# Probabilities turned in float32r after a copy by DMA, and weight sums formed on loading, in a two-layer encoder on one Trainium2 core

## The chip, the cores and the metric

The kernel runs on one NeuronCore of one Trainium2 chip. The metric is the device time of one execution in microseconds (us), median over runs. TensorE (PE) multiplies and transposes and its weight loads are shown as PEld; VectorE (DVE), ScalarE (ACT) and GpSimd (POOL) work on elements; SyncE (SP) issues most transfers, POOL the others, and 16 DMA engines carry them out. SP's transfers run on the queue that the profile calls hardware_dynamic (q1), POOL's on software_dynamic (q0).

## The reference, cut to what matters

Two layers, sequence 1024, width 1024, all in float32.

```python
def block_attention(q, k, v, scale):          # in 128-query blocks
    s = jnp.einsum('bqhgd,bkhd->bhgqk', qi, k) * scale
    p = jax.nn.softmax(s, axis=-1)
    return jnp.einsum('bhgqk,bkhe->bqhge', p, v)

def conv_gated_ffn(h, w_up, conv_w, conv_b, w_down):
    a = h @ w_up                              # 1024 x 1024 by 1024 x 5632
    a = ap[:, :-2] * conv_w[0] + ap[:, 1:-1] * conv_w[1] + ap[:, 2:] * conv_w[2] + conv_b
    gate, val = a[..., :D_FF], a[..., D_FF:]
    return (jax.nn.silu(gate) * val) @ w_down # 1024 x 2816 by 2816 x 1024

for l in range(DEPTH):
    x = x + hybrid_mixer(rms_norm(x), ...)    # 6 heads GQA, 6 heads MLA, gMLP, then w_out
    x = x + memory_cross_attention(rms_norm(x), mem, ...)
    x = x + conv_gated_ffn(rms_norm(x), ...)
return rms_norm(x)
```

## The kernel before, in words

All large products are made in float32r, which TensorE multiplies faster than float32 but with fewer bits. Each operand is therefore split into a rounded part (`hi`) and the rest (`lo`), and a product is the sum of three matmuls (hi hi, hi lo, lo hi). Work tiles are 46 slots of 128 x 1024 elements in the on-chip memory; `Slots` hands them out from a list, first in, first out, at the time the program is written, so the code's order decides which tile takes which slot. A tile that gets a slot waits until the last readers and writers of that slot's former tile are done. Each engine runs its instructions in the order of the code.

**Attention** (about 172 to 500 us in the first layer and 1550 to 1860 us in the second). There are 24 items in a layer, numbered 0 to 23: 12 heads by two halves of 512 queries. An item has four tiles of 128 queries by 1024 keys. The function `attention` runs one step for each tile. In step s of item i it issues: the scores of tile s (TensorE, L318 and L319, or L744 and L745) and their maximum (VectorE, L295); the scaling of the tile before by the reciprocal of its sum (POOL, L305); two `turn` calls for the item before; then the exponential of tile s (ScalarE, L299). `turn(k)` transposes the k-th 128 keys of all four tiles into one bank of the accumulator memory (TensorE, L140, four transposes by a float32 identity `ident`) and splits that bank (ScalarE hi, L123, VectorE lo, L124); `value(k)` multiplies the two parts with the values. With `LAG = 1` the first `turn` of an item comes one step after the step in which the scaling of its fourth tile is issued. Side work (`fill`) and transfers (`extra`, by item number) are placed between these.

**Weight sums.** The up and down products of the feed-forward are made by a scheme of seven products of half size in place of eight (Strassen's kind), numbered m = 1 to 7. The weight is stored as four blocks w0 to w3; products 1, 2 and 4 take a block as it is, and 5, 7, 6 and 3 take the sums w2+w3, w0+w2, w0+w2+w3 and w0+w1+w2+w3. In the kernel before, all four sums are formed in DRAM while attention runs: a copy on SP's queue (`copy`, L796) and an adding transfer on POOL's queue (`add`, L801), piece by piece, and the last additions for the down weights during the up projection (`add_later`).

**Up projection** (about 746 to 1165 us in the first layer). `order` lists (j, m): column block j of 22 and product m. For each the loop calls `fetch` (a 256 KB block into half a slot, SP, L1089), `make_w` (hi by ScalarE, L1096, lo by VectorE, L1097), `product` (12 matmuls, L1143 to L1145) and `post`. Fetching runs nine products ahead (`FETCH`) and splitting four (`AHEAD`). The convolution and gate follow in small steps (`todo`); `keep(j)` stores the result in DRAM (`gq`, SP, L1213) and forms the sums of row blocks by adding transfers on POOL's queue (L1216).

**Down projection.** `fetch_d` loads the block of kept rows and that of the weight, `make_d` splits both, `d_mm` multiplies (L1256).

Other lines named below: L110 is the rounding in `load` (POOL), L132 the power in `rstd` (POOL), L688 a sum over partitions with one moving column, L116 to L118 are the three matmuls of `mm3`.

Of the kernel before, what the change touches and what calls it, by code (L numbers as in the profile page):

```python
# [35 lines left out]
LAG = 1  # L36
WARM = 16
# [32 lines left out]
def trunk(ctx: ExitStack, tc: tile.TileContext, a: dict, out: bass.AP):  # L70
# [3 lines left out]
    stats = ctx.enter_context(tc.tile_pool(name="stats", bufs=24))  # L74
# [8 lines left out]

    def ins_of(i):
        return getattr(i, 'ins', i)
# [13 lines left out]
    ident = cpool.tile([P, P], F32, name="ident")  # L99
    ones = cpool.tile([P, 1], F32, name="ones")  # L100
# [34 lines left out]
    def transpose4(srcs):  # L135

        b = bank()
        for j, s in enumerate(srcs):
            m = s.shape[-1]
            nc.tensor.transpose(b[:m, j * P : (j + 1) * P], s, ident)  # L140
        return b
# [139 lines left out]
    class Item:  # L281
# [20 lines left out]
        def scale(self, t):  # L302
            p, r = self.ps[t], stat()
            nc.vector.reciprocal(r[:, 0:1], self.den[:, t : t + 1])  # L304
            Item.last = nc.gpsimd.tensor_scalar(p, p, r[:, 0:1], 0.0, ALU.mult, ALU.add)  # L305
# [78 lines left out]
    def layer(l, nt, w_m, last):  # L384
# [396 lines left out]
        class Blocks:  # L781

            def __init__(self, w, parts, name):
                self.w, self.parts, self.at = w, parts, [sum(parts[:i]) for i in range(len(parts))]
                self.sum = {
                    (m, i): dpool.tile([P, n * CH + 16], F32, tag=f"{name}{l}_{m}_{i}", name=f"{name}{l}_{m}_{i}")[:, : n * CH]
                    for m in (5, 6, 7, 3) for i, n in enumerate(parts)
                }  # L790
# [4 lines left out]
            def copy(self, m, i):  # L795
                c = nc.sync.dma_start(self.sum[m, i], self.piece({5: 2, 6: 0, 7: 0, 3: 1}[m], i))  # L796
                tc.add_manual_dep(ins_of(c), ins_of(Item.last).name, mybir.DependencyInfo(mybir.DependencyClass.Sync, mybir.DependencyReason.DATA), reason="not sooner")

            def add(self, m, i):
                src = self.sum[{6: 5, 3: 6}[m], i] if m in (6, 3) else self.piece({5: 3, 7: 2}[m], i)  # L800
                tc.keep_in_program_order(nc.gpsimd.dma_start(self.sum[m, i], src, accum_op=ALU.add))  # L801

            def block(self, m, j):
                if m in (1, 2, 4):
                    return self.w[{1: 0, 2: 1, 4: 3}[m]][:, j * CH : (j + 1) * CH]
                i = max(i for i in range(len(self.parts)) if self.at[i] <= j)
                return self.sum[m, i][:, (j - self.at[i]) * CH : (j - self.at[i] + 1) * CH]

            def steps(self):
                n = len(self.parts)  # L810
                return [(self, m, i + o) for i in range(0, n, 2) for m, o in ((5, 0), (5, 1), (7, 0), (6, 0), (6, 1), (7, 1), (3, 0), (3, 1)) if i + o < n]
# [5 lines left out]
        items += [mla(h, c) for h in range(MLA_H) for c in range(NC)]  # L817
        fill[0] += [lambda k=k: turn_cq(0, k) for k in range(2)] + [lambda: norm_low(1, ssq)]
# [51 lines left out]
        extra, steps = {}, w_u.steps()  # L870
        for n, (w, m, i) in enumerate(steps):
            g = n * 18 // len(steps)
            extra.setdefault(g, []).append(lambda w=w, m=m, i=i: w.copy(m, i))
            extra.setdefault(g + 3, []).append(lambda w=w, m=m, i=i: w.add(m, i))
        later = deque(sorted(w_d.steps(), key=lambda s: (5, 7, 6, 3).index(s[1])))
        for n, (w, m, i) in enumerate(later):
            extra.setdefault(n * 20 // len(later), []).append(lambda w=w, m=m, i=i: w.copy(m, i))

        def add_later():
            if later:  # L880
                w, m, i = later.popleft()
                w.add(m, i)
# [218 lines left out]
        for _ in range(FETCH - AHEAD):  # L1101
            fetch()
# [107 lines left out]
        def keep(j):  # L1210
# [4 lines left out]
            for q, p in ((("u3", "22"), ("u2", "u1"), ("u4", "u2")) if j % 2 else (("u1", "11"),)):  # L1215
                nc.gpsimd.dma_start(gq[q, i], gq[p, i], accum_op=ALU.add)  # L1216
# [6 lines left out]
        def fetch_d():  # L1223
            if (mi := next(d_fetch, None)) is not None:
# [3 lines left out]
                nc.sync.dma_start(quarter(z, 1), w_d.block(m, i))  # L1228
# [35 lines left out]
        def down(after0, after1, tail):  # L1264

            for m, i in d_order:
# [20 lines left out]
                for _ in range(2):  # L1287
                    if todo:
                        todo.popleft()()
                if i == NP - 1:  # L1290
# [8 lines left out]
        for i, (j, m) in enumerate(order):  # L1299
            for _ in range(1 + (i < AHEAD)):  # L1300
                fetch()
            for _ in range(1 + (i < AHEAD)):
                make_w()
# [6 lines left out]
            if m == 5 and j > 1:  # L1310
# [93 lines left out]
    nc.sync.dma_start(ident, a["ident"])  # L1404
    nc.sync.dma_start(colts[0], a["cols"][0])
# [96 lines left out]
```

## Time and profile before

| | |
|---|---|
| median of 3 runs | 2774.91 us (2772.91 to 2776.51) |
| the profiled execution | 2770.64 us, its span 2768.8 us |
| granted TensorE clock | 0.998 of full speed |
| busy share PE, PEld, DVE, ACT, POOL | 98%, 83%, 70%, 53%, 26% |
| DMA queues q1 (SP) and q0 (POOL) | 323.84 MB and 92.28 MB |
| transposes of `transpose4` (L140) | 2320, 324.0 us busy |

The span is the profiled execution from its first to its last instruction; all sums of durations are held against it. A row of groups reads: line, engine, operation, out<-in with buffer numbers left out, count, then busy us and mean ns of one. Matmul durations overlap, so the time from one start to the next is what a matmul costs in a row of them. The chain of waits is the path of work that ended last, followed back from the end. In the windows, each engine's busy us stand in a stretch of 50 us, then the granted clock, the DMA engines' mean busy share and GB/s. A slot is `s` in all rows; `u` and `d` are the weight sums in DRAM, `g` (also `g_u`) the kept rows, `stat` small columns, `bank` and `pair` accumulators.

### The profile page before, as it was taken

The numbers are of one execution on the slowest core, as the hardware profiler recorded it, in microseconds if no ns is written. First come the engines' busy times: TensorE is split into PE (matmuls) and PEld (weight loads), VectorE is DVE, ScalarE is ACT, GpSimd is POOL, SyncE is SP. The second block draws the span as 40 slices with busy tenths as digits, with TensorE's granted clock in tenths as the row PEclk, the third lists the DMA queues.
The fourth block names the chain that finished last, engine by engine and source line by source line (L and its number), as shares of the span: only waits on it lengthen the run. The fifth ranks groups of instructions, "written<-read, shape, count | busy, mean of one in ns | idle before, by whom it ended". The sixth has DMA issues, their size and how long they took to land.

```text
span 2768.8 us, 37951 instructions
## 1 busy us (share of the span) xinstructions
PE 2724.2 (98%) x13648; PEld 2284.4 (83%) x13648; DVE 1941.6 (70%) x2905; ACT 1470.8 (53%) x2838; POOL 706.3 (26%) x744
## 2 busy tenths in 40 slices
PE   9999999999999999999999999999999999999998
PEld 7997888888878888888889877888888888888887
DVE  5489879556697777774445888894666877778754
ACT  4378978224554444553333888881345544446432
POOL 3245676320001110000123456662200011100000
PEclk9999999999999999999999999999999999999999
DMA  4027994221159875785210289831221698767752
GB/s 147 27 80 199 263 233 97 73 69 62 46 150 237 223 213 166 225 272 183 88 59 19 83 232 265 220 83 61 70 68 46 173 239 225 204 169 244 247 187 102
DMA packets 160748, 418.80 MB, mean 151 GB/s; under 512 B 17840, under 2 KB 18480, under 8 KB 146224
## 3 DMA queue, kind: packets, MB, share of 16 engines
q1 hardware_dynamic: 137376, 323.84, 34.6%
q0 software_dynamic: 23040, 92.28, 18.2%
q8 instruction: 107, 1.75, 0.2%
q14 instruction: 81, 0.66, 0.1%
q10 hardware_dynamic: 144, 0.26, 0.0%
HBM read 371.75 MB, written 206.05 MB: 209 GB/s over the span
## 4 chain that ended last, share of the span: by engine, by line
PE 85%; DVE 5%; ACT 3%; DMA 3%; POOL 2%; issue 1%; SPq 0%; POOLq 0%; DVEq 0%; ACTq 0%
PE bank L1256 8%; PE bank L116 7%; PE bank L118 7%; PE bank L117 7%; PE bank L140 7%; PE pair L1256 6%; PE bank L1144 5%; PE bank L1145 5%; PE bank L1143 5%; PE pair L1143 4%; PE pair L1144 4%; PE pair L1145 4%; PE bank L318 3%; PE bank L319 3%; PE pair L116 2%; PE pair L118 2%
## 5 line engine op out<-in xcount | busy, mean ns | idle before, releaser
L124 DVE TENSOR_TENSOR s<-bank,s 128x512 fp32r<-128x512 f32 (+3 forms) x552 | 331.5, 630 | 116.4 <-ACT s L123 112.7
L116 PE MATMUL bank<-s,s 128*128 128x512 f32 (+4 forms) x1124 | 404.2, 360 | 4.6 <-DVE s L124 3.4
L118 PE MATMUL bank<-s,s 128*128 128x512 f32 (+4 forms) x1124 | 399.5, 356 | 1.1 <-DVE s L111 0.9
L117 PE MATMUL bank<-s,s 128*128 128x512 f32 (+4 forms) x1124 | 398.4, 355 | 0.3 <-DVE s L111 0.3
L123 ACT ACTIVATE s<-bank 128x512 fp32r<-128x512 f32 (+3 forms) x552 | 286.0, 556 | 205.7 <-PE bank L140 142.5
L140 PE MATMUL bank<-ident,s 128*128 128x128 f32 (+1 forms) x2320 | 324.0, 274 | 17.5 <-POOL s L305 6.3
L140 PEld LDWEIGHTS bank<-ident,s 128*128 128x128 f32 (+1 forms) x2320 | 270.1, 140 | 77.7 <-DVE s L124 9.6
L1096 ACT ACTIVATE s<-s 128x512 fp32r<-128x512 f32 x308 | 187.5, 627 | 181.5 <-PE bank L1145 46.1
L1144 PE MATMUL bank<-s,s 128*128 128x512 f32 x704 | 274.5, 390 | 0.9 <-DVE s L209 0.9
L1145 PE MATMUL bank<-s,s 128*128 128x512 f32 x704 | 273.9, 389 | 0.0
L1143 PE MATMUL bank<-s,s 128*128 128x512 f32 x704 | 273.7, 389 | 0.0
L305 POOL TENSOR_SCALAR s<-s,stat 128x1024 f32<-128x1024 f32 x192 | 222.8, 1160 | 184.4 <-DVE stat L304 136.5
L295 DVE TENSOR_REDUCE stat<-pair 128x1 f32<-128x1024 f32 x192 | 233.5, 1216 | 39.6 <-PE pair L118 19.0
L132 POOL TENSOR_TENSOR stat<-stat,mhalf 128x1 f32<-128x1 f32 (+3 forms) x94 | 84.3, 897 | 634.3 <-DVE stat L131 634.1
L1256 PE MATMUL bank<-s,s 128*128 128x512 f32 (+1 forms) x1068 | 242.7, 387 | 1.6 <-DVE stat L131 1.6
L116 PEld LDWEIGHTS bank<-s,s 128*128 128x128 f32 x1124 | 211.7, 189 | 33.6 <-DVE s L124 3.7
L1241 DVE TENSOR_TENSOR s<-s,s 128x512 fp32r<-128x512 f32 x264 | 170.6, 685 | 93.1 <-ACT s L1240 93.1
L1256 PEld LDWEIGHTS bank<-s,s 128*128 128x128 f32 x1068 | 198.7, 188 | 42.3 <-DVE x L1347 1.8
L118 PEld LDWEIGHTS bank<-s,s 128*128 128x128 f32 x1124 | 211.7, 188 | 26.3 <-DVE s L111 1.3
L117 PEld LDWEIGHTS bank<-s,s 128*128 128x128 f32 x1124 | 212.1, 189 | 24.1 <-DVE s L111 0.6
L1240 ACT ACTIVATE s<-s 128x512 fp32r<-128x512 f32 x264 | 153.9, 623 | 140.9 <-DMA s<-g_u 47.3
L1097 DVE TENSOR_TENSOR s<-s,s 128x512 fp32r<-128x512 f32 x308 | 201.7, 686 | 36.2 <-ACT s L1096 33.9
(182 smaller groups left out, 5521.0 us busy)
## 6 DMA issues: line engine op xcount, KB each, us to landing
s<-u SPq DMA_DIRECT2D x176, 256.0 KB, 4.3
u<-in_w_up SPq DMA_DIRECT2D x40, 1024.0 KB, 13.3
s<-in_w_up SPq DMA_DIRECT2D x132, 256.0 KB, 4.4
g_u<-s SPq DMA_DIRECT2D x88, 256.0 KB, 3.0
s<-g_u SPq DMA_DIRECT2D x88, 256.0 KB, 3.3
s<-d SPq DMA_DIRECT2D x88, 256.0 KB, 3.6
u<-in_w_up POOLq DMA_DIRECT2D x20, 1024.0 KB, 18.4
u<-u POOLq DMA_DIRECT2D x20, 1024.0 KB, 13.3
```

Of the source, the lines that this page charges most:

```text
L116: nc.tensor.matmul(o, l[0], r[0], start=first, stop=False)
L117: nc.tensor.matmul(o, l[0], r[1], start=False, stop=False)
L118: nc.tensor.matmul(o, l[1], r[0], start=False, stop=last)
L123: nc.scalar.activation(hi, src, AF.Copy)
L124: nc.vector.tensor_tensor(lo, src, f(hi), ALU.subtract)
L140: nc.tensor.transpose(b[:m, j * P : (j + 1) * P], s, ident)
L295: nc.vector.reduce_max(self.nm[:, 0:1], s, axis=AX.X, negate=True)
L305: Item.last = nc.gpsimd.tensor_scalar(p, p, r[:, 0:1], 0.0, ALU.mult, ALU.add)
L1143: nc.tensor.matmul(o, lh, rh, start=k == 0 and m in (1, 5, 6), stop=False, skip_group_check=True)
L1144: nc.tensor.matmul(o, lh, rl, start=False, stop=False, skip_group_check=True)
L1145: nc.tensor.matmul(o, ll, rh, start=False, stop=k == 3, skip_group_check=True)
L1256: nc.tensor.matmul(o, lh[p], rh[q], start=m in (1, 5, 2) and i == 0 and k == 0, stop=i == NP - 1 and k == 2, skip_group_check=True)
```

## The change

- In 18 of 24 items (`BY_DMA`: 0 to 10 and 17 to 23) the tiles t = 0, 1, 2 are copied, after scaling, by a transfer on SP's queue into a fresh slot of type float32r (512 KB, 54 in each layer). The old slot goes back to the list at once. Transposes of these tiles use the float32r identity `identr` and write float32r; the fourth tile of each item, and all tiles of items 11 to 16, stay float32.
- Of the weight sums only w0+w2+w3 (m = 6) is formed in DRAM, by a copy that is now on POOL's queue and two additions. Sums for m = 5, 7 and 3 are formed on loading: SP loads the first block (256 KB) and POOL issues an adding transfer of the second into the same half slot, 66 times in each up projection and 33 times in each down projection.
- Before the up projection `AHEAD` = 4 blocks are fetched in place of `FETCH - AHEAD` = 5. The adding transfers of `keep` are put off by 3, 6 and 9 products (`due`). `add_later` is called for even j only and has six additions in place of its earlier ones. The pool of small columns has 23 buffers in place of 24.

```diff
+BY_DMA = (*range(0, 11), *range(17, 24))
...
-    stats = ctx.enter_context(tc.tile_pool(name="stats", bufs=24))
+    stats = ctx.enter_context(tc.tile_pool(name="stats", bufs=23))
...
+    identr = cpool.tile([P, P], F32R, name="identr")
...
-            nc.tensor.transpose(b[:m, j * P : (j + 1) * P], s, ident)
+            o = b[:m, j * P : (j + 1) * P]
+            if s.dtype == F32R:
+                nc.tensor.transpose(o.bitcast(F32R), s, identr)
+            else:
+                nc.tensor.transpose(o, s, ident)
...
-            Item.last = nc.gpsimd.tensor_scalar(p, p, r[:, 0:1], 0.0, ALU.mult, ALU.add)
+            nc.gpsimd.tensor_scalar(p, p, r[:, 0:1], 0.0, ALU.mult, ALU.add)
+            if self.by_dma and t < TPC - 1:
+                w = self.ps[t] = sl.get()
+                nc.sync.dma_start(f(w), p)
+                sl.put(p)
...
-            def copy(self, m, i):
-                c = nc.sync.dma_start(self.sum[m, i], self.piece({5: 2, 6: 0, 7: 0, 3: 1}[m], i))
...
+            def copy(self, i):
+                tc.keep_in_program_order(nc.gpsimd.dma_start(self.sum[i], self.piece(0, i)))
+            def add(self, i, b):
+                tc.keep_in_program_order(nc.gpsimd.dma_start(self.sum[i], self.piece(b, i), accum_op=ALU.add))
...
+            def load(self, z, m, j):
+                first, *second = {1: (0,), 2: (1,), 4: (3,), 6: (4,), 5: (2, 3), 7: (0, 2), 3: (4, 1)}[m]
+                nc.sync.dma_start(z, self.col(first, j))
+                if second:
+                    nc.gpsimd.dma_start(z, self.col(second[0], j), accum_op=ALU.add)
...
+        for i in range(len(UP_PARTS)):
+            extra.setdefault(2 * i, []).append(lambda i=i: w_u.copy(i))
+            for n in range(2):
+                extra.setdefault(2 * i + 4 + 3 * n, []).append(lambda i=i, n=n: w_u.add(i, 2 + n))
+        for i in range(len(DOWN_PARTS)):
+            extra.setdefault(13 + 2 * i, []).append(lambda i=i: w_d.copy(i))
...
-                nc.sync.dma_start(raws[jm][0], w_u.block(jm[1], jm[0]))
+                w_u.load(raws[jm][0], jm[1], jm[0])
...
-        for _ in range(FETCH - AHEAD):
+        for _ in range(AHEAD):
             fetch()
...
-                nc.gpsimd.dma_start(gq[q, i], gq[p, i], accum_op=ALU.add)
+                due.append((step[0] + 3 + 3 * n, lambda q=q, p=p, i=i: nc.gpsimd.dma_start(gq[q, i], gq[p, i], accum_op=ALU.add)))
...
-                nc.sync.dma_start(quarter(z, 1), w_d.block(m, i))
+                w_d.load(quarter(z, 1), m, i)
...
-            if m == 5 and j > 1:
+            if m == 5 and j > 1 and j % 2 == 0:
                 add_later()
...
+    nc.vector.tensor_copy(identr, ident)
```

SP in the attention of the first layer, around items 8 and 9. Names are `s<slot>_<use>_<number>` for slots, `u0_` and `d0_` for pieces of the sums; what an instruction waits for stands in brackets, by semaphore (DMAHW for transfers on hardware queues, DMASW for those of POOL's). Before:

```order
L796 DMA d0_7_1_1640<-in_w_down 128x2048 [waits DMAHW6_49]
L796 DMA u0_7_2_1623<-in_w_up 128x2048 [waits DMAHW7_49,Pool_49]
L796 DMA u0_6_2_1617<-in_w_up 128x2048 [waits DMAHW0_49,Pool_49]
L796 DMA d0_7_2_1641<-in_w_down 128x2048 [waits DMAHW1_49]
L796 DMA u0_6_3_1618<-in_w_up 128x2048 [waits DMAHW2_49,Pool_49]
```

After:

```order
L311 DMA s45_279_3050<-s2_277_3030 128x1024 [waits DMAHW0_49,PE_49,Pool_49]
L311 DMA s3_284_3091<-s27_282_3068 128x1024 [waits PE_49,Pool_49]
L311 DMA s14_288_3128<-s2_287_3109 128x1024 [waits DMAHW2_49,DMAHW6_49,PE_49,Pool_49]
L311 DMA s6_297_3199<-s42_294_3179 128x1024 [waits DMAHW3_49,PE_49,Pool_49]
L311 DMA s35_302_3237<-s25_300_3217 128x1024 [waits DMAHW4_49,PE_49,Pool_49]
```

The copies of weights are gone from this queue and copies of tiles stand there, each behind a scaling on POOL.

ScalarE at the same place, before (exponentials are L299, splits L123):

```order
L123 ACTIVATE s42_259_3087<-bank_3082 128x512 [waits PE_49]
L299 ACTIVATE s4_261_3098,stat_2996<-pair_3072,stat_3077 128x1024 [waits DVE_49,Activation_49]
L123 ACTIVATE s24_260_3095<-bank_3090 128x512 [waits PE_49]
L123 ACTIVATE s2_262_3123<-bank_3118 128x512 [waits PE_49,Activation_49]
L123 ACTIVATE s6_263_3131<-bank_3126 128x512 [waits PE_49,Activation_49]
L299 ACTIVATE s9_264_3134,stat_2996<-pair_3108,stat_3113 128x1024 [waits DVE_49,Activation_49]
```

After (L302 and L122):

```order
L122 ACTIVATE s38_290_3143<-bank_3138 128x512 [waits PE_49,Pool_49]
L302 ACTIVATE s2_287_3109,stat_3003<-pair_3081,stat_3086 128x1024 [waits DMAHW0_49,DVE_49]
L302 ACTIVATE s29_291_3146,stat_3003<-pair_3118,stat_3123 128x1024 [waits DMAHW7_49,DVE_49]
L122 ACTIVATE s27_292_3168<-bank_3163 128x512 [waits DMAHW1_49,PE_49,Pool_49]
L122 ACTIVATE s34_293_3176<-bank_3171 128x512 [waits PE_49]
L302 ACTIVATE s42_294_3179,stat_3152<-pair_3153,stat_3158 128x1024 [waits DVE_49]
```

Slot 2, read by the copy `s45_279_3050<-s2_277_3030`, is written next by the exponential `s2_287_3109`, which now waits for that copy.

POOL at the start of the up projection, before:

```order
L110 TENSOR_SCALAR s16_663_7287<-s27_662_7286 128x1024 [waits DMAHW5_49,DVE_49,PE_49]
L132 TENSOR_TENSOR stat_7443<-stat_7442,mhalf_77 128x1 [waits DVE_49]
L132 TENSOR_TENSOR stat_7453<-stat_7452,mhalf_77 128x1 [waits DVE_49]
L132 TENSOR_TENSOR stat_7489<-stat_7488,mhalf_77 128x1 [waits DVE_49]
L132 TENSOR_TENSOR stat_7525<-stat_7524,mhalf_77 128x1 [waits DVE_49]
```

After (rows 306 to 310 of POOL), and further on in the projection (rows 326 to 332):

```order
L817 DMA s5_752_7872<-in_w_up 128x512 [waits DMAHW4_49,PE_49]
L817 DMA s5_752_7872<-in_w_up 128x512 [waits DMAHW5_49,DMASW6_49]
L131 TENSOR_TENSOR stat_7485<-stat_7484,mhalf_78 128x1 [waits DVE_49]
L131 TENSOR_TENSOR stat_7495<-stat_7494,mhalf_78 128x1 [waits DVE_49]
L131 TENSOR_TENSOR stat_7531<-stat_7530,mhalf_78 128x1 [waits DVE_49]
```

```order
L1223 DMA g0_u1_0_7828<-g0_11_0_7795 128x512 [waits DMAHW3_49,DMAHW2_49,DMASW1_49]
L817 DMA s41_815_8378<-in_w_up 128x512 [waits DMASW2_49,DMAHW5_49,DVE_49,Activation_49]
L817 DMA s6_823_8461<-in_w_up 128x512 [waits DMAHW1_49,PE_49,Pool_49]
L1223 DMA g0_u3_0_7850<-g0_22_0_7817 128x512 [waits DMAHW4_49,DMAHW2_49,DMASW4_49]
L1223 DMA g0_u2_0_7839<-g0_u1_0_7828 128x512 [waits DMAHW5_49,DMASW5_49,DMASW1_49]
L817 DMA s5_828_8505<-in_w_up 128x512 [waits DMAHW4_49,DMAHW3_49,DMAHW7_49,DMASW6_49,DVE_49]
L1223 DMA g0_u4_0_7861<-g0_u2_0_7839 128x512 [waits DMASW7_49,DMASW5_49]
```

The accumulates of weights (L817) now stand ahead of the powers and between the accumulates of kept rows, of which u2 and u4 wait for another accumulate.

More of the change, by code (lines that the diff above doesn't have):

```diff
@@ L82, in f @@
         return ap.bitcast(F32) if ap.dtype == F32R else ap
-    def ins_of(i):
-        return getattr(i, 'ins', i)
     def stat():
@@ L786, in __init__ @@
                 self.w, self.parts, self.at = w, parts, [sum(parts[:i]) for i in range(len(parts))]
[L787 to L790, printed above, removed]
+                self.sum = [dpool.tile([P, n * CH + 16], F32, tag=f"{name}{l}_{i}", name=f"{name}{l}_{i}")[:, : n * CH] for i, n in enumerate(parts)]
@@ L792, in piece @@
             def piece(self, b, i):
                 return self.w[b][:, self.at[i] * CH : (self.at[i] + self.parts[i]) * CH]
-            def copy(self, m, i):
[L796 to L801, printed above, removed]
@@ L803, in block @@
-            def block(self, m, j):
-                if m in (1, 2, 4):
-                    return self.w[{1: 0, 2: 1, 4: 3}[m]][:, j * CH : (j + 1) * CH]
-                i = max(i for i in range(len(self.parts)) if self.at[i] <= j)
[L807 to L811, printed above, removed]
+            def copy(self, i):
+                tc.keep_in_program_order(nc.gpsimd.dma_start(self.sum[i], self.piece(0, i)))
@@ L817, in layer @@
         items += [mla(h, c) for h in range(MLA_H) for c in range(NC)]
+        for i, o in enumerate(items):
+            o.by_dma = i in BY_DMA
         fill[0] += [lambda k=k: turn_cq(0, k) for k in range(2)] + [lambda: norm_low(1, ssq)]
@@ L867, in layer @@
         fill[23] += [lambda: y_split(1, 1, 2)]
[L870 to L877, printed above, removed]
+        extra, later = {}, deque((w_d, i, b) for b in (2, 3) for i in range(len(DOWN_PARTS)))
+        for i in range(len(UP_PARTS)):
[4 more added lines that the diff above has]
+            extra.setdefault(13 + 2 * i, []).append(lambda i=i: w_d.copy(i))
         def add_later():
             if later:
-                w, m, i = later.popleft()
-                w.add(m, i)
+                w, i, b = later.popleft()
+                w.add(i, b)
         w_o = {}
@@ L1214, in keep, with add_due @@
             sl.put(z)
-            for q, p in ((("u3", "22"), ("u2", "u1"), ("u4", "u2")) if j % 2 else (("u1", "11"),)):
-                nc.gpsimd.dma_start(gq[q, i], gq[p, i], accum_op=ALU.add)
+            for n, (q, p) in enumerate((("u3", "22"), ("u2", "u1"), ("u4", "u2")) if j % 2 else (("u1", "11"),)):
+                due.append((step[0] + 3 + 3 * n, lambda q=q, p=p, i=i: nc.gpsimd.dma_start(gq[q, i], gq[p, i], accum_op=ALU.add)))
+        due, step = deque(), [0]
+        def add_due(all=False):
+            while due and (all or due[0][0] <= step[0]):
+                due.popleft()[1]()
         NP = NF // 2
@@ L1289, in down @@
                         todo.popleft()()
+                step[0] += 1
+                add_due(not todo)
                 if i == NP - 1:
@@ L1299, in layer @@
         for i, (j, m) in enumerate(order):
+            step[0] = i
             for _ in range(1 + (i < AHEAD)):
                 fetch()
+            add_due()
             for _ in range(1 + (i < AHEAD)):
```

4 lines of the change are left out of this document (added).

## The prediction

> **What bounds the kernel now.** I read the page's totals first, then the chain of waits by engine, then windows inside the two stages that the change touches, then single rows there.
>
> ```profile
> span 2768.8 us, 37951 instructions
> PE 2724.2 (98%) x13648; PEld 2284.4 (83%) x13648; DVE 1941.6 (70%) x2905; ACT 1470.8 (53%) x2838; POOL 706.3 (26%) x744
> PE 85%; DVE 5%; ACT 3%; DMA 3%; POOL 2%; issue 1%; SPq 0%; POOLq 0%; DVEq 0%; ACTq 0%
> ```
>
> TensorE is busy for 98% of the span and carries 85% of the chain. On that average any time taken from TensorE would be time saved. The windows say otherwise for the stage in which the transposes lie (the first three rows are attention in the first layer, the last four its up projection):
>
> ```profile
> core 0: us, PE busy (x) PEld busy (x) DVE busy (x) ACT busy (x) POOL busy (x), PEclk, DMA share, GB/s
> 200.00:250.00 50.00, 49.19 (x279) 39.63 (x278) 45.18 (x86) 44.16 (x90) 27.58 (x27) 1.00 0.63 166
> 250.00:300.00 50.00, 48.41 (x282) 39.25 (x282) 44.76 (x78) 43.46 (x87) 34.87 (x40) 1.00 0.88 236
> 300.00:350.00 50.00, 49.19 (x277) 39.96 (x276) 43.29 (x70) 46.61 (x95) 32.29 (x34) 1.00 1.01 268
> 800.00:850.00 50.00, 50.00 (x223) 41.37 (x222) 37.07 (x50) 22.46 (x34) 7.90 (x10) 1.00 0.96 257
> 850.00:900.00 50.00, 48.48 (x213) 39.61 (x212) 38.80 (x51) 23.70 (x34) 7.10 (x9) 1.00 0.90 220
> 900.00:950.00 50.00, 50.00 (x221) 41.18 (x221) 34.73 (x45) 22.60 (x32) 6.63 (x8) 1.00 0.88 228
> 1000.00:1050.00 50.00, 50.00 (x221) 40.96 (x220) 37.04 (x47) 24.16 (x33) 4.93 (x6) 1.00 0.76 198
> ```
>
> In attention VectorE works 43 to 45 of 50 us and ScalarE 43 to 47: both stand close behind TensorE, so a gain there stops after some tenths of its size. In the up projection TensorE has no gap and the DMA engines are at 0.76 to 0.96. The chain inside attention shows the same: for 11.3 us it runs on ScalarE and VectorE alone, between these rows.
>
> ```profile
> 246.92 1.24 DVE stat L295
> 248.18 1.21 ACT s L299 x2
> ...
> 257.51 0.70 DVE s L124
> 258.25 0.66 PE bank L140 x4
> ```
>
> **The transposes.** 18 items x 3 tiles x 8 = 432 transposes in each layer go from float32 to float32r, 864 in all. Their price now, and the rows nearest to their price then (the chain, then the timeline of TensorE):
>
> ```profile
> 238.80 1.09 PE bank L140 x8
> 242.05 0.44 PE bank L140 x4
> 386.82 1.68 PE bank L688 x16
> 601.94 0.28 PE L116 MATMUL bank<-s,s 128*128 128x256 f32 x1
> 603.61 0.28 PE L118 MATMUL bank<-s,s 128*128 128x256 f32 x1
> 802.09 0.23 PE pair L1143
> 804.58 0.24 PE pair L1145
> ```
>
> Four float32 transposes in 0.44 us make 0.109 us each. No float32r transpose is in the trace. The narrowest float32r products move 256 columns and follow each other at (603.61 - 601.94)/14 = 0.119 us; those of 512 columns at (804.58 - 802.09)/11 = 0.226 us, so 256 columns more cost 0.107 us. Two ends follow. If 128 columns less save half of that, a transpose takes 0.066 us and TensorE is spared 864 x 0.043 = 37 us. If it takes as long as the 256-column product, the change costs 864 x 0.010 = 9 us. Between them stands the L688 row: one moving column each, yet 1.68/16 = 0.105 us, as if something other than the columns set the pace.
>
> The Trainium skill has a rule for that row: by "TensorE: Matmul & The Clock Gate", section "LDWEIGHTS (loading the stationary operand)", a weight load takes the number of its columns over 1.2 ns, 107 ns for 128, whatever is moved. The L688 row agrees with it; if it holds for the float32r transposes, their term below is 0 in place of -12 us and the sum 12 us higher.
>
> I take 0.066 us, the value on the line through the two float32r rows, which are the same kind of product, but count only a third of the 37 us as saved, because VectorE and ScalarE have but 3 to 7 us of 50 left: **-12 us**, range -37 to +9.
>
> **The copies.** 54 copies of 512 KB in each layer lie between ScalarE's exponential, POOL's scaling and the transposes. SP issues them between the loads (0.5 us each, by the first row below). The first tile of an item has three steps of the loop in which to land and the second two (a step is 328 us of attention over 24 items of 4 steps, 3.4 us), the third has only one. Third scaling and first transpose of the third tile are shown for the first and the last of the 36 items and for the tightest one; the third matmul of the row is meant (the second in the first item):
>
> ```profile
> 303.93 0.49 SPq L796 DMA_DIRECT2D u<-in_w_up  x1
> 175.16 1.14 POOL L305 TENSOR_SCALAR s<-s,stat 128x1024 f32<-128x1024 f32 x1 [1.24 <-DVE stat L304]
> 178.75 0.49 PE L140 MATMUL bank<-ident,s 128*128 128x128 f32 x3
> 465.61 1.11 POOL L305 TENSOR_SCALAR s<-s,stat 128x1024 f32<-128x1024 f32 x1
> 468.28 0.49 PE L140 MATMUL bank<-ident,s 128*128 128x128 f32 x3
> 1866.80 1.12 POOL L305 TENSOR_SCALAR s<-s,stat 128x1024 f32<-128x1024 f32 x1
> 1870.47 1.04 PE L140 MATMUL bank<-ident,s 128*128 128x128 f32 x8
> ```
>
> From the end of the scaling these are 2.6, 1.8 and 2.8 us; over the 36 the median is 3.15 us. No copy within the on-chip memory is in the trace. The nearest are transfers of the same size one way, and of half the size (the page's issues, median from issue to landing):
>
> ```profile
> s<-in_w_up SPq DMA_DIRECT2D x132, 256.0 KB, 4.4
> g<-s SPq DMA_DIRECT2D x66, 256.0 KB, 2.2
> g_u<-g POOLq DMA_DIRECT2D x44, 256.0 KB, 5.5
> g_u<-g_u POOLq DMA_DIRECT2D x44, 256.0 KB, 5.5
> s<-in_w_out SPq DMA_DIRECT2D x16, 512.0 KB, 3.4
> out_dram<-s SPq DMA_DIRECT2D x7, 512.0 KB, 2.9
> ```
>
> Summing over the 36 items by how much a copy outlasts its gap gives 0.4 us for a copy of 2.0 us, 7 for 2.9, 16 for 3.4, 27 for 3.9, 41 for 4.4. I take 3.4, the row measured amid other traffic: **+16 us**, range 0 to 41. TensorE waits in its own order, so scores and weighted sums behind those transposes wait too.
>
> Each copy also holds the slot it reads until it has landed, while the list gives that slot out again 5 to 20 requests later. In the order 110 rows of ScalarE in the attention of both layers wait for a copy or load on a hardware queue, where 13 did. An item takes 13.7 us (328 us of attention over 24 items) and makes some 17 requests, so 5 requests are 4 us: the shortest reuses meet a copy that is not done, and what stands behind on ScalarE is the split that TensorE waits for. A tenth of the 110 at 0.7 us: **+8 us**, range 0 to 40.
>
> **The sums in memory.** The page's queues give a rate: 34.6% and 18.2% of the span, over their bytes, are 2.96 and 5.46 us for a MB.
>
> ```profile
> q1 hardware_dynamic: 137376, 323.84, 34.6%
> q0 software_dynamic: 23040, 92.28, 18.2%
> ```
>
> Of each attention 34.6 MB of copies on SP's queue vanish (102 us of DMA work) and POOL's queue goes from 23.1 MB of additions to 20.2 MB of additions and copies (16 us less); the copies of tiles, 28.3 MB, put 84 us back. I cost the relief at nothing: no sum was waited for there, and SP's queue gets copies in place of copies.
>
> **The loads that sum.** In the up projection 66 of 154 blocks in a layer become a load of 4.4 us, an issue on POOL and an accumulate that I price like those above.
>
> ```profile
> 303.83 0.83 POOL L801 DMA_DIRECT2D u<-in_w_up  x1
> 823.37 11.63 DMA g_u<-s
> 836.00 9.63 DMA s<-in_w_up
> ```
>
> That is 4.4 + 0.8 + 5.5 = 10.7 us. A product is twelve matmuls at the 0.226 us above, 2.72 us, and the fetch, now four products ahead (five before), leads by 10.9 us. The margin is 0.2 us, and two rows of the chain, a load of 9.6 us and a store of 11.6, show that transfers here do run long. Besides, POOL's queue holds two accumulates of kept rows in each 14 products (u2 and u4) that wait for another accumulate, with the weight accumulates behind them. The DMA work: in the first 260 us of the stage 41 accumulates of 0.262 MB add 41 x 0.262 x 5.46 = 59 us, the halved additions for the down weights take away 31; on a mean share of 0.875 that makes (228 + 28)/260 = 0.98. What covers this is the second lead: a block, once there, is cast four products before its use, so ScalarE can be 8 us late before TensorE stops, and it has 26 of 50 us free. Low end 0; high end 44 such holds x 5.5 us less what ScalarE's lead takes up, a third, 80 us. I take 8 us for each layer, **+16 us**, near the low end because the cover is 8 us deep and the stage had a row at 0.96 with TensorE at 50.00.
>
> At the start of that projection POOL has two accumulates ahead of seven powers and four ahead of the eighth, each behind a load: 4.4 us at most once a layer, and half of that reaches the end: **+4 us**, range 0 to 10. In the down projection 33 blocks a layer get the same chain under the same lead, at nothing: one of two loads of each block was already there, and nothing but TensorE is near full.
>
> Sum against the profiled run (2770.64 us, span 2768.8): -12 + 16 + 8 + 16 + 4 = +32, 2803 us. That run is 4.3 us below the median of 2774.91 us, so the forecast is **2807 us**; about 0.2% (5.5 us) is what a measurement can tell from no change.
>
> **Rivals.**
> (a) The accumulates come late as a rule: DMA work over 1.0 in the first 100 us of the up projection (0.93 + 0.11) builds a backlog that outgrows the 8 us cover. Then the up term is its 80, the time 2871 us. Against it: the mean of 0.98 lets a backlog drain.
> (b) The other side: copies land in 2.4 us or less (shortfall 2 us) like the 2.2 us row, the accumulates stay inside both leads, and two thirds of the 37 us of shorter transposes arrive, because ScalarE and VectorE then catch up in the stretches in which TensorE is the later one: 2775 - 24 = 2751 us. For it: two DMA rows near that price and less DMA work in attention; the point of decision is the third copy's landing at about 2.5 us. Against: DMA at 0.88 to 1.01 there.
> (c) The change doesn't do what it says: transposes stay at 0.105 us and the waits are hidden, 2775 us. The L688 row speaks for the pace, nothing for the cover. The rule of the Trainium skill named above would give this time, if the waits hide.
> (d) Waits of about half my terms, 2787 us.
>
> **Chances.** My forecast 0.48 (its own range 2793 to 2845 us), (a) 0.13, (b) 0.25, (c) 0.07, (d) 0.07. Faster comes from (b), 0.25; the same from (c), 0.07; slower from the rest, 0.68. The range leaves out (a)'s upper part and (b)'s lower: 2742 to 2868 us.
>
> **What would show it.** In the profile after: the pitch of the float32r transposes (0.066 or 0.105 us); TensorE's idle time before them put down to a DMA into a slot, 16 us or so over the 36 items; ScalarE waiting for DMA before the exponential and the hi half; accumulates into slots with 5.5 us, and ScalarE's cast waiting for them without TensorE stopping much. A landing of the copies near 2 us, or accumulates far above 5.5 us, would make the prediction wrong.

## The result, and the profile after

The changed kernel takes 2929.25 us (median of 4 runs, 2926.39 to 2935.28), the kernel before 2773.92 us on the same chip: a ratio of 1.0563, with a 95% interval of 1.0551 to 1.0576. That is 155 us slower; the forecast was 2807 us, and the time lies 61 us above the upper end of the range.

The totals of the page, after (span, busy time of the engines, kinds of DMA transfers with KB and median us from issue to landing):

```profile
span 2926.2 us, 38660 instructions
PE 2760.1 (94%) x13648; PEld 2287.9 (78%) x13648; DVE 1943.5 (66%) x2906; ACT 1467.2 (50%) x2838; POOL 862.6 (29%) x924
...
s<-in_w_up SPq DMA_DIRECT2D x220, 256.0 KB, 4.7
s<-s SPq DMA_DIRECT2D x108, 512.0 KB, 3.1
s<-in_w_up POOLq DMA_DIRECT2D x132, 256.0 KB, 5.6
```

The medians are the ones forecast: a copy of a tile 3.1 us (3.4 was taken), an accumulate into a slot 5.6 (5.5 was taken). They do not show where 155 us went. The lengths of the stages do. Windows over the two attentions and the two up projections, each from its first instruction to its last, before and after:

```profile
165.10:522.10 357.00, 347.72 (x1986) 287.44 (x1985) 300.84 (x496) 286.08 (x589) 213.53 (x215) 1.00 0.66 175
745.70:1174.90 429.20, 425.80 (x1880) 348.82 (x1879) 328.05 (x440) 214.34 (x311) 43.97 (x53) 1.00 0.73 199
1539.10:1896.60 357.50, 349.11 (x1982) 288.49 (x1982) 301.04 (x495) 286.29 (x589) 214.32 (x216) 1.00 0.66 175
2121.20:2550.10 428.90, 426.24 (x1880) 348.74 (x1879) 327.88 (x440) 214.14 (x311) 43.93 (x53) 1.00 0.73 199
```

```profile
165.30:562.60 397.30, 357.75 (x1984) 285.57 (x1983) 304.13 (x495) 286.30 (x589) 209.03 (x213) 0.96 0.45 134
786.40:1257.30 470.90, 435.95 (x1880) 352.56 (x1879) 326.51 (x440) 213.00 (x311) 97.19 (x112) 0.98 0.85 206
1621.40:2015.70 394.30, 356.94 (x1984) 286.41 (x1983) 304.03 (x495) 285.77 (x589) 209.04 (x213) 0.95 0.45 135
2240.10:2707.50 467.40, 435.07 (x1880) 352.72 (x1879) 325.34 (x440) 212.60 (x311) 97.28 (x112) 0.98 0.85 208
```

The second number is the length of the stage. Attention grew by 40.3 and 36.8 us, the up projections by 41.7 and 38.5, together 157.3 us, the whole difference of the spans; every other stage kept its length to 1 us. Two further readings: the DMA engines have less to do in attention than before (0.45 in place of 0.66), and the granted TensorE clock, 1.00 before, is 0.95 to 0.98. Lost clock makes 17 and 19 us of the attentions and 9 us of each up projection (one minus the clock times the length), about 53 us in all. That is an upper end: where the half-clock time in which TensorE stood idle anyway is left out, some 46 us remain.

What TensorE waited for, over the whole run after (waits: us in total, times, longest us):

```profile
PE bank L141 <- DMA s<-s: 44.8, 21, 3.3
PE pair L1150 <- DVE s L1178: 34.9, 14, 7.9
PE pair L1150 <- DVE s L1176: 24.6, 12, 4.7
```

The longest total before, and the one before of the up projection, were

```profile
PE bank L140 <- POOL s L305: 6.3, 4, 2.5
PE pair L1143 <- DVE s L1171: 2.0, 2, 1.5
```

Of the rows after, the first is the copies (L141 is the float32r transpose). The other two are in the up projections: not a missing block, but accumulators that VectorE's additions (L1176, L1178) had not yet read. One item of attention shows the first, item 4 of the first layer, in the timeline (start, us, engine and line):

```profile
233.49 0.87 POOL L804 DMA_DIRECT2D u<-in_w_up  x1
234.08 0.83 POOL L801 DMA_DIRECT2D u<-in_w_up  x1
236.26 0.47 SPq L311 DMA_DIRECT2D s<-s  x1
245.05 0.28 PE L141 MATMUL bank<-identr,s 128*128 128x128 f32 x1 [2.98 <-DMA s<-s]
```

Two transfers of 1 MB for the weight sums are issued 2.8 and 2.2 us ahead of the copy of the third tile. That copy lands 8.74 us after its issue, at 245.00, and TensorE starts 0.05 us later. Of the 36 third copies 12 took more than 8 us, each with one or two such transfers issued in the 4 us before it; of the 18 third copies that met none in flight, 14 took 2.85 to 3.2 us and the longest 5.3. SP is not what delays them: each third copy is issued 0.03 us after its scaling ends. The windows behind that wait show its second price:

```profile
240.00:244.00 4.00, 2.06 (x11) 1.35 (x9) 2.25 (x6) 2.55 (x5) 2.13 (x2) 1.00 0.99 388
244.00:248.00 4.00, 2.40 (x11) 1.76 (x11) 1.67 (x3) 1.97 (x5) 1.37 (x2) 0.72 0.61 248
248.00:252.00 4.00, 3.95 (x14) 3.02 (x14) 2.90 (x8) 3.18 (x8) 1.13 (x1) 0.50 0.10 39
252.00:256.00 4.00, 4.00 (x27) 3.28 (x25) 2.82 (x5) 1.80 (x3) 0.03 (x1) 0.93 0.25 96
```

After 3 us of idleness the clock stands at 0.50 for 6.8 us (245.7 to 252.6), in which 14 matmuls pass in 4 us where 27 do at full clock.

### The profile page after: what moved, and what is told of

The parts are those of the page before. It is cut to its first block, busy times and chain, and to the rows that moved or that the text cites. A ratio compares the mean times of both kernels' runs of the same rounds, so it can differ in the third digit from the quotient of the medians.

```text
span 2926.2 us, 38660 instructions
## 1 busy us (share of the span) xinstructions
PE 2760.1 (94%) x13648; PEld 2287.9 (78%) x13648; DVE 1943.5 (66%) x2906; ACT 1467.2 (50%) x2838; POOL 862.6 (29%) x924
## 5 line engine op out<-in xcount | busy, mean ns | idle before, releaser
L123 DVE TENSOR_TENSOR s<-bank,s 128x512 fp32r<-128x512 f32 (+3 forms) x552 | 330.7, 631 | 155.4 <-ACT s L122 152.7
L122 ACT ACTIVATE s<-bank 128x512 fp32r<-128x512 f32 (+3 forms) x552 | 284.6, 556 | 243.3 <-PE bank L143 147.0
L1104 DVE TENSOR_TENSOR s<-s,s 128x512 fp32r<-128x512 f32 x308 | 208.4, 688 | 170.9 <-ACT s L1103 168.5
L1150 PE MATMUL pair<-s,s 128*128 128x512 f32 x528 | 214.3, 406 | 61.5 <-DVE s L1178 34.9
L143 PE MATMUL bank<-ident,s 128*128 128x128 f32 (+1 forms) x1456 | 248.6, 282 | 9.2 <-DVE s L150 3.2
L115 PEld LDWEIGHTS bank<-s,s 128*128 128x128 f32 x1124 | 211.8, 189 | 33.5 <-DVE s L123 4.2
L302 ACT ACTIVATE s<-pair,stat 128x1024 f32<-128x1024 f32 x192 | 214.5, 1118 | 38.5 <-DMA s<-s 20.0
L1255 DVE TENSOR_TENSOR s<-s,s 128x512 fp32r<-128x512 f32 x264 | 170.5, 687 | 94.2 <-ACT s L1254 93.9
L117 PEld LDWEIGHTS bank<-s,s 128*128 128x128 f32 x1124 | 212.0, 189 | 26.3 <-DVE s L110 1.6
L1270 PEld LDWEIGHTS bank<-s,s 128*128 128x128 f32 x1068 | 198.8, 188 | 42.3 <-DVE x L1365 1.9
L817 POOL DMA_DIRECT2D s<-in_w_up x132 | 121.0, 971 | 376.1 <-DMA s<-in_w_up 115.9
```

What stands on the lines that cost most here:

```text
L115: nc.tensor.matmul(o, l[0], r[0], start=first, stop=False)
L117: nc.tensor.matmul(o, l[1], r[0], start=False, stop=last)
L122: nc.scalar.activation(hi, src, AF.Copy)
L123: nc.vector.tensor_tensor(lo, src, f(hi), ALU.subtract)
L143: nc.tensor.transpose(o, s, ident)
L1150: nc.tensor.matmul(o, lh, rh, start=k == 0 and m in (1, 5, 6), stop=False, skip_group_check=True)
```

## The experiments

Theory: attention loses by third copies that stand behind 1 MB transfers, and by the clock after each such wait; the up projections lose because a summed block comes too late for a lead of four products, and the waiting cast (ScalarE, then VectorE) holds the additions behind it that free accumulators. Rivals: the order of the sums on POOL's queue as such, slots held by copies, the DMA engines' whole time, the deferred additions of kept rows. Stage lengths below are first layer / second layer.

**No copies.**

```diff
-BY_DMA = (*range(0, 11), *range(17, 24))
+BY_DMA = ()
```

> The changed kernel with no item copied (all probabilities transposed in float32 from their own slots); the sums are still formed on loading. Theory: the attention loss (40.3 us in the first layer, 36.8 in the second, from stage marks of the two traces) comes from the copies alone, so attention returns to 357 us a layer and only the 80 us of the up projections stay: 2845 to 2860 us. Rival: the copy of the weight sums that is now on POOL's queue, or POOL's queue as such, slows attention: then 2875 us or more.

Measured: 2843.51 us (ratio to before 1.0256, 1.0226 to 1.0285). Attention 353.4 / 353.5 us, up projections 466.9 / 472.8. The row of the first attention:

```profile
165.20:518.60 353.40, 347.92 (x1984) 287.51 (x1983) 301.95 (x495) 285.62 (x589) 206.82 (x213) 1.00 0.29 71
```

The copies carry all of the attention loss; without them attention is 4 us shorter than before. That the smaller DMA share (0.29 in place of 0.66) is worth these 4 us is not shown: the last kernel below has a share of 0.28 and takes 358.4 us.

**No sum in DRAM.**

```diff
-            extra.setdefault(2 * i, []).append(lambda i=i: w_u.copy(i))
-                extra.setdefault(2 * i + 4 + 3 * n, []).append(lambda i=i, n=n: w_u.add(i, 2 + n))
-            extra.setdefault(13 + 2 * i, []).append(lambda i=i: w_d.copy(i))
...
-                first, *second = {1: (0,), 2: (1,), 4: (3,), 6: (4,), 5: (2, 3), 7: (0, 2), 3: (4, 1)}[m]
+                first, *second = {1: (0,), 2: (1,), 4: (3,), 6: (0,), 5: (2, 3), 7: (0, 2), 3: (0, 1)}[m]
```

> The changed kernel without the m = 6 sum in DRAM (no copy, no addition during attention nor of the down weight later; products 6 and 3 take block 0 instead, so that part is left out), with the 108 copies of tiles kept. Theory: a copy takes 2.85 us and becomes 8 to 11 us only behind a 1 MB transfer of POOL's queue; without these all 36 third tiles land in about 3 us, TensorE's wait for copies falls from 44.8 to under 10 us, attention to 348 to 360 us a layer, total 2835 to 2860 us. Rival (slot reuse: ScalarE and VectorE wait for slots that copies hold): attention stays above 375 us a layer, total over 2890 us.

Measured: 2849.56 us. None of the 108 copies takes over 8 us (12 did), the longest 4.9; attention is 370.7 / 364.6 us, so the 1 MB transfers cost 27 / 30 us of it. But 17 / 11 us over the kernel without copies stay, and attention is above the theory's 360: the copies cost something by themselves. TensorE's largest waits in the first attention are now these two, POOL's scaling of the uncopied fourth tile, and copies:

```profile
PE bank L143 <- POOL s L308: 6.3, 4, 2.4
PE bank L141 <- DMA s<-s: 5.7, 4, 2.8
```

The up projections fell too, to 449.4 / 460.4. This kernel also leaves out the additions for the down weights in them; that these are the reason is not shown. Without that fall, of 28 us together, the total would lie above the theory's range, so that it lies inside is luck.

**Copies, but float32.**

```diff
-                w = self.ps[t] = sl.get()
+                w = self.ps[t] = sl.get(F32)
```

> The changed kernel with the copies kept but into float32 slots, so that all transposes are float32 (0.109 us in place of 0.060 us apart). Theory: the shorter transposes bring little where copies are waited for: 5 to 25 us more than the changed kernel, 2935 to 2955 us. Rival: they bring all of 864 x 0.049 = 42 us, 2965 us or more; second rival: nothing, since VectorE and ScalarE set the pace, 2926 to 2932 us.

Measured: 2936.22 us (2933.1 to 2939.34). Attention is 393.8 / 397.9 us, 791.7 together, against 791.6 with float32r: in this kernel the shorter transposes bring nothing that shows (one attention is 3.5 us shorter, the other 3.6 us longer), as the second rival had it. The total lies just inside the theory's range, but not by the theory's cause: the extra time is in the up projections (465.9 / 476.5 against 470.9 / 467.4), which the edit does not touch.

**Sums after the third copy.**

```diff
-            if s == 2 and g < n:
+            if s == 3 and g < n:
                 for step in extra.get(i, ()):
```

> The changed kernel with the transfers of the weight sums issued one step of attention later, after the copy of the third tile instead of just before it; nothing else moves. Theory: the third copies land in 2.9 to 4 us again and the first tile of the next item, which has 10 us, pays little: attention falls by 25 to 40 us a layer, total 2850 to 2880 us. Rival: the 16 DMA engines are short of time in attention wherever the sums stand: the first and second tiles wait instead and the total stays above 2910 us.

Measured: 2908.72 us. Attention 384.8 / 387.7, 12.5 / 6.6 us less, a third of what was expected. Copies over 8 us fell from 12 to 6 of 108; the transfers now meet other tiles' copies, and waits remain on TensorE (first attention):

```profile
PE bank L141 <- DMA s<-s: 15.1, 11, 3.5
```

and, for slots under copy, on ScalarE:

```profile
ACT s L302 <- DMA s<-s: 10.4, 5, 3.3
ACT s L122 <- DMA s<-s: 5.3, 3, 3.3
```

**No accumulates on loading.**

```diff
-                if second:
-                    nc.gpsimd.dma_start(z, self.col(second[0], j), accum_op=ALU.add)
```

> The changed kernel with the 198 accumulates on loading left out (products 5, 7 and 3 take only their first block). Theory: the up projections lose their 80 us against the kernel before because a summed block reaches ScalarE 12.8 us after its load is issued (median) and not 4.7; without accumulates they take 429 us each again and the total is 2845 to 2860 us. Rival: the deferred additions of kept rows or the shorter fetch lead cost it: then the up projections stay above 450 us.

Measured: 2854.24 us, up projections 431.1 / 430.8: all but 2 us of the loss in each is the accumulates, by their lateness or by their bytes. The row of the first:

```profile
787.50:1218.60 431.10, 426.16 (x1880) 348.92 (x1879) 327.18 (x440) 214.97 (x311) 38.87 (x47) 1.00 0.67 186
```

The deferred additions and the shorter prefetch, which this kernel keeps, cost no more than that.

**Blocks fetched seven products ahead.**

```diff
-AHEAD, FETCH = 4, 9
+AHEAD, FETCH = 2, 9
...
-        for _ in range(AHEAD):
+        for _ in range(FETCH - AHEAD):
             fetch()
```

> The changed kernel with weight blocks fetched seven products before their cast and cast two products before their use (four and four in the changed kernel): the same transfers and bytes. Theory (the chain of load and accumulate is too long for a lead of 10.9 us, and a cast that waits holds VectorE's additions that free the accumulators): a lead of 19 us covers the 12.8 to 17 us of the chain, the up projections fall from 471 and 467 us to 430 to 445 us, total 2865 to 2895 us. Rival (the DMA engines, at 0.88 to 0.92 of their time there, are the limit): no more than 10 us are won, 2915 us or more. Second rival: two products between cast and use are too few, and TensorE waits for VectorE: above 2930 us.

Measured: 2884.73 us, up projections 446.3 / 443.8, 24 us less each with the same bytes:

```profile
787.00:1233.30 446.30, 428.60 (x1880) 349.83 (x1879) 329.26 (x441) 212.87 (x313) 93.73 (x109) 1.00 0.87 214
```

So lateness, not the whole time of the DMA engines, made three fifths of the loss. The waits of ScalarE's cast on blocks in the first up projection (from 786.40 us) were, in the changed kernel,

```profile
ACT s L1103 <- DMA s<-in_w_up: 110.8, 31, 10.9
```

and VectorE stood behind them, with TensorE behind VectorE:

```profile
DVE s L1104 <- ACT s L1103: 82.2, 54, 8.0
```

```profile
PE pair L1150 <- DVE s L1178: 19.1, 8, 7.7
PE pair L1150 <- DVE s L1176: 12.3, 6, 3.3
```

With the longer lead the cast waits

```profile
ACT s L1103 <- DMA g_u<-s: 25.5, 12, 6.6
ACT s L1103 <- DMA s<-in_w_up: 7.9, 2, 4.5
```

and TensorE

```profile
PE pair L1150 <- DVE s L1178: 14.1, 6, 3.2
PE pair L1150 <- DVE s L1176: 1.7, 1, 1.7
```

The first row of the cast is not among its longer waits in the changed kernel: stores of kept rows (`g_u<-s`), by the code out of the slot that the cast is to write. What it costs by itself was not tested.

**Both moves.** The edits of the last but one kernel on attention (sums one step later) and of the last together.

> The changed kernel with both moves together: weight sums issued after the third copy, and weight blocks fetched seven products ahead of the cast. Theory (two separate stages, two separate causes): the gains add, 2929 - 20 - 44 = 2865 us, between 2855 and 2875 us. Rival (the gains share a cause in the DMA engines): 2880 us or more.

Measured: 2862.54 us: the gains add (2929 - 20 - 44 = 2865), as two stages with separate causes would have it.

**Slots given back later.** On the kernel with the sums after the third copy:

```diff
+            while len(Item.held) > 1:
+                sl.put(Item.held.popleft())
             p, r = self.ps[t], stat()
...
-                sl.put(p)
+                self.held.append(p)
```

> The kernel with the sums after the third copy (2908.7 us), and each slot that a copy reads goes back to the list two scalings later, some 7 us, so that it has landed before the slot can be given out. Theory: what is left of the attention loss is in good part ScalarE waiting for slots under copy (10.4 + 5.3 us in the first layer), so attention falls by 5 to 12 us a layer, 2885 to 2900 us. Rival: those waits lie beside other waits, and the total stays between 2903 and 2914 us.

Measured: 2896.9 us, attention 378.0 / 380.9, 6.8 us less in each. The waits of ScalarE for a slot under copy are gone from its list; TensorE's wait for copies stays (13.9 us in the first attention). Slots under copy are a real, smaller part; the edit also changes which tile takes which slot.

**Float32r without copies.** On the kernel before, with `identr` and `transpose4` of the change; POOL's scaling rounds the probabilities to float32r, in all items and tiles.

```diff
-            Item.last = nc.gpsimd.tensor_scalar(p, p, r[:, 0:1], 0.0, ALU.mult, ALU.add)
+            w = self.ps[t] = sl.get()
+            Item.last = nc.gpsimd.tensor_scalar(w, p, r[:, 0:1], 0.0, ALU.mult, ALU.add)
+            sl.put(p)
```

> The kernel before with no copies and all sums in DRAM, but POOL's scaling writes its result into a float32r slot (all four tiles, all items), which rounds the probabilities, and all of their transposes are float32r. TensorE is spared 768 x 0.049 = 37 us in each attention. Theory: VectorE (43 to 45 of 50 us) and ScalarE (43 to 47) take over as the bound, and 3 to 12 us a layer arrive: 2750 to 2768 us. Rival: most of it arrives (25 us or more a layer): under 2725 us. Second rival: nothing arrives, 2770 to 2778 us.

Measured: 2783.35 us (8 runs), ratio 1.0036, 1.0025 to 1.0047: 9 us slower, outside both the theory and the rivals. TensorE is spared work, and the attention does not get shorter (first and second):

```profile
165.50:526.40 360.90, 338.65 (x1985) 275.50 (x1984) 301.71 (x495) 285.93 (x589) 215.22 (x215) 1.00 0.66 173
1545.30:1908.40 363.10, 340.51 (x1983) 276.15 (x1982) 302.00 (x495) 285.67 (x589) 215.13 (x216) 0.99 0.66 172
```

In the first, TensorE's busy time falls from 347.7 to 338.7 us while the stage grows from 357.0 to 360.9. The trace shows where the expected 37 us went. Neighbouring transposes start 0.06 or 0.085 us apart, about equally often, and the matmul behind a row of them starts 0.093 us after the last one, where 0.036 us was enough behind float32 ones. Summed from each transpose's start to the start of what follows it (leaving out what follows a wait), they take 71.2 us where they took 85.9, so that some 15 us are spared. TensorE's idle time, the stage less the busy time, grows from 9.3 to 22.3 us and takes nearly all of that back. The longest of these waits are

```profile
PE bank L143 <- POOL s L311: 5.0, 4, 2.3
PE bank L143 <- DVE s L125: 4.9, 7, 1.4
PE pair L751 <- ACT s L304: 2.4, 6, 0.6
```

so that TensorE waits for the three engines behind it; which of them sets the pace was not tested. Nor was the reason for the 4 to 6 us more; the edit also makes each tile hold a second slot for a while.

**Copies with the old sums.** On the kernel before, only the copies and their transposes added (the `scale` and `transpose4` of the change).

> The kernel before (all four sums in DRAM, as before) with only the copies of tiles and the float32r transposes added. Theory: up projections are back at 429 us, and in attention the copies meet twice the 1 MB transfers, on both queues, so attention loses as much as in the changed kernel or more, 395 to 430 us a layer: 2850 to 2920 us. Rival: the copies are only slow behind POOL's queue in its new order; attention at 357 to 375 us, 2775 to 2810 us.

Measured: 2967.39 us, attention 456.5 / 452.5, up projections 429.0 / 428.5. With 60 transfers for the weight sums in each attention, where the changed kernel has 21, 35 of 108 copies take over 8 us (longest 20.9), TensorE waits 54.9 us for copies in the first attention up to 580 us, and its clock in that attention is 0.90:

```profile
PE bank L144 <- DMA s<-s: 54.9, 13, 12.5
```

This is worse than expected, and it shows what the change of the sums was good for: with the copies in place it saves some 59 us in each attention.

**Two tiles in place of three.** Both moves, slots given back later, and `t < TPC - 2`.

> The kernel with both moves (2862.5 us), with slots under copy given back two scalings later, and only the first two tiles of the 18 items copied; the third stays float32 in its slot. Theory: the third copy, with a gap of some 3 us, and the slots under copy are what is left of the attention loss (384.6 and 385.5 us against 357): attention falls to 353 to 365 us a layer, the total to 2800 to 2825 us, and not below, since the shorter transposes bring nothing. Rival (a copy costs by itself, by its place in SP's queue and in the slots): attention stays above 370 us a layer, total above 2833 us.

Measured: 2823.47 us, attention 362.5 / 363.4. No wait for a copy is left among TensorE's larger ones. Two hidden copies for each item still give 9 us more than the kernel without copies (353.4), but only 4 to 5 us more than the next kernel, which also has no copies and issues the sums one step later, as this one does (358.4). What these few us are was not tested; the place in SP's queue is not it, as the median copy is issued 0.03 us after its scaling and the latest 0.17.

**The best of this kind.** No copies, `AHEAD, FETCH = 2, 11` with `FETCH - AHEAD` blocks fetched ahead of the projection, `step[0] + 8 + 3 * n`, sums one step later.

> A version meant to be the best of this kind: no tile copied, sums of three weights formed on loading, blocks fetched nine products ahead of a cast that is two products ahead of its use, additions of kept rows put off by five products more, weight sums issued one step later. Theory: attention 353 us a layer (it lost 4 us of 357 with the sums gone), up projections 430 to 440 us: 2770 to 2790 us, about the time before. Rival: the DMA engines or POOL's queue, whose waits are in order, keep the up projections at 446 us: 2800 us or more.

Measured: 2792.12 us, ratio 1.007, 1.0053 to 1.0087; attention 358.4 / 358.4, up projections 436.7 / 437.9. Just above the theory's 2790, with the up projections as expected and attention 5 us over them. The reason for these 5 us was not tested. No kernel of this study beats the kernel before.

## Why the prediction was wrong

The direction and the stages were right: copies late for the third tile, slots under copy, late summed blocks. The sizes were not: the terms came to +32 us and the run shows +155.

- **Transposes, -12.** The commonest pitch was right: neighbouring float32r transposes start 0.06 us apart most often, near the 0.066 of the line through the 256- and 512-column products, not 0.105. But two steps failed. The first is 864 times that gain: the mean pitch of neighbours is 0.080 us in the first attention after, and what follows a float32r transpose in the mixed rows starts 0.09 to 0.10 us after it. Summed as for the kernel without copies, all transposes of the two attentions take 85.9 and 85.8 us before and 77.8 and 77.0 us after, half clock included: 17 us are spared, not 37. The second is "a third arrives": none does, by the kernel with float32 copies and by the one without copies. That VectorE and ScalarE, at 43 to 47 of 50 us, are what holds it back is argued from their busy shares; the waits name POOL as well. The L688 row was a false neighbour. By the Trainium skill, "TensorE: Matmul & The Clock Gate", section "LDWEIGHTS (loading the stationary operand)", 128 columns take 107 ns; here transposes with a load of 128 columns each follow at 60 ns, so the measurement decides against its use as a pace.
- **Third copy, +16.** The step that failed is taking one duration, 3.4 us, for all 36. The median is 4.3 us, near enough, but the sum is made by 12 copies of 8 to 11 us, against gaps of about 3. The prediction had counted the DMA work as a mean share, put the copies into it, and costed the remaining sums at nothing, while the order of the code puts the 1 MB transfers just ahead of the third copy in each item. Measured: 27 / 30 us for the meeting with the transfers, 17 / 11 us for the copies without it, slots included. The tightest gap was misread too: item 9 has 1.3 us in both layers, not 1.8, which would have made the term 19 us and changes little.
- **The clock, not in the sum.** A wait was priced at its own length. Most waits of 2 to 3 us in attention were followed by 3.4 or 6.8 us at half the clock, the longest of the up projections (7.7 and 8.0 us) went with 10.2, in the clock's record always in steps of 3.41 us. That is 46 to 53 us in all; it is a part of the sizes measured for the other terms, not beside them. The Trainium skill, in "TensorE: Matmul & The Clock Gate", section "Part 1: The HAM clock gate (the "warmup" mystery)", has the clock halved after one idle window of about 3.4 us and freed after a busy one; the trace agrees in the state (0.50) and in the step (3.41 us), and shows it after waits below 3.4 us as well (2.98 us here, 1.63 us at 1746.0 us), while waits of 1.78 us at 225.8 us and of 2.29 us at 1029.8 us passed without it. So the length of a wait alone does not tell whether the clock falls.
- **Slots under copy, +8.** Right in kind: 6.8 us in each attention by the kernel that gives slots back later, 14 us for both, measured with the sums one step later.
- **Relief of DMA work, 0.** No worth is shown: the two kernels without copies and with this relief have attentions of 353.4 and 358.4 us, 4 us shorter and 1 us longer than before.
- **Loads that sum, +16.** Measured 80 (accumulates 40 / 37 by leaving them out). Two steps failed. The chain was built from medians, 10.7 us against a lead of 10.9; in the trace after it is 13.0 us in the median of 132 from issue of the load to landing of the accumulate, and 15.4 or more for the slowest tenth. Load and accumulate take their 4.7 and 5.6 us; what the sum of medians left out is that waits add up, and that 52 of the 132 accumulates were issued more than 1 us after their load had landed, up to 5.2, on POOL's queue, where accumulates of kept rows wait 114.2 us for their stores in the first up projection, with those of the weights behind them. And the "second lead", 8 us of cover between a cast and its product, did not protect TensorE: a block is indeed cast some 20 us before its product in the trace, but a waiting cast stops ScalarE's and then VectorE's queue, and behind it stand the additions that free accumulators for the very next products. The row of a stage with TensorE at 50.00 beside a DMA share of 0.96 said that bytes were no limit, not that a wait in VectorE's queue would be free.
- **Start of the up projection, +4.** About nothing: VectorE waits 4.2 us for the eighth power in each layer, but TensorE's wait behind that is 0.6 us. The down projections, put at nothing, kept their length to 1 us.

Rival (a) named the right stage for the second half, with the price of its upper end, 80 us, but for a backlog of bytes; the longer lead, with the same bytes, took 24 of 40 us away. That the 80 met the measured 80 is luck: the cut of 44 x 5.5 us to a third of it had no row behind it. Rival (b) had copies land in 2.4 us or less; the fastest of the 108 took 2.84 us, and the slow ones decide. Rivals (c) and (d) had the waits hidden or halved, and they were several times the terms.

## What to carry to other kernels

A transfer put on the path must be priced by what else is issued in the microseconds before it, not by its median: read the order of the queues around each issue, and the largest transfers first. A lead between stages counts only if nothing that the next stage needs stands behind the waiting instruction in its engine's queue. A pitch between neighbouring instructions is not yet a saving: sum the whole rows in which they stand. And where TensorE is the bound, a wait may cost up to about twice its length, by the clock that follows it: here 2.98 us of idleness were followed by 6.8 us at half clock, which is up to 3.4 us more.

## What the runs showed of the hardware

- A copy of 512 KB within the on-chip memory takes 2.85 us from issue to landing at best (14 of the 18 third copies that met no transfer for the weight sums took 2.85 to 3.2 us), and up to 10.7 us behind one or two 1 MB transfers of the other queue. The Trainium skill, "DMA: Bandwidth & Descriptors", section "Queues, rings and completion order", says that each DMA engine takes turns between its queues, packet by packet; by that a copy that shares with one transfer would take about twice its 2.85 us, an estimate of 6 us. The eight third copies behind one transfer took 3.4 to 9.0 us, the ten behind two 8.7 to 10.7: the estimate holds for some of those behind one; how the packets were cut is not known.
- Neighbouring float32r transposes of 128 x 128 start 0.06 us apart most often, and 0.085 us about as often in the kernel that has only these, where float32 ones start 0.109 us apart.
- In the changed kernel, after waits of TensorE of 1.6 to 3.3 us its clock often stood at 0.50 for 3.41 or 6.83 us; after others of 1.8 and 2.3 us it did not.
